# Row-wise largest magnitude on one core: two load queues, a ring of six slots, a finer tail and a direct last store

## The chip, the cores and the metric

One core of a Trainium2 chip runs the whole program. The metric is device time in microseconds (us) per execution. All times compared here are of the fast state, at full granted clock; experiments 8 and 9 are single runs of unknown state, read only for the stores inside them. "Span" is the time covered by the profiled execution; the time of an execution reads 1.7 to 1.9 us more (2.0 to 2.1 in experiment 4).

## The reference

```python
"x": np.random.randn(8192, 8192).astype(np.float32)

def reference(x):
    return np.linalg.norm(x, ord=np.inf, axis=1)      # largest |x| of each row
```

268 MB go in, 32 KB come out. There is one pass over the data and nothing is used twice.

## The kernel before

The 8192 rows form 64 tiles of 128 rows, one row per partition. Below, "row t" means tile t: 128 x 8192 values, 4 MB.

```python
COOLDOWN = ([[4096, 4096]] * 7 + [[4096, 2048, 2048]]
    + [[2048, 2048, 2048, 2048]] + [[2048, 2048, 1536, 1280, 1280]])
...
    chunks = [[n_cols]] * (T - len(COOLDOWN)) + COOLDOWN
...
pool = ctx.enter_context(tc.tile_pool(name="sbuf", bufs=5))
...
    for h, w in enumerate(ch):
        dst = res[:, t : t + 1] if len(ch) == 1 else partial[:, h : h + 1]
        nc.sync.dma_start(out=xt[:, off : off + w], in_=x_t[t, :, off : off + w])
        nc.vector.tensor_reduce(out=dst, in_=xt[:, off : off + w], ...,
            op=mybir.AluOpType.max, apply_absolute_value=True)
        off += w
    if len(ch) > 1:
        nc.vector.tensor_reduce(out=res[:, t : t + 1], in_=partial[:, : len(ch)], ...)
...
nc.tensor.transpose(res_t_psum, res, ident)           # 128 x 64 -> 64 x 128
nc.vector.tensor_copy(out=res_t, in_=res_t_psum)
nc.sync.dma_start(out=out.rearrange("(t p) -> t p", p=P), in_=res_t)
```

SP (SyncE) issues every load. The last ten rows come in pieces, so that little is left to reduce when the last bytes land. All results leave in one store at the end.

## Time and profile before

| | before |
|---|---|
| time, median | 634.63 us (634.53 to 634.78, 4 runs) |
| span | 632.9 us |
| one row arrives every | 9.71 us |
| one row takes VectorE (DVE) | 8.69 us |
| last reduce ends / span ends | 629.33 / 632.9 |

A list of DMA issues by output and input gives the time from issue to landing in its last column. For the final store of before it has:

```profile
out_dram<-res_t SPq DMA_DIRECT2D x1, 32.0 KB, 1.8
```

That is 64 rows of 512 B in 1.8 us.

### The profile page before, as it was taken

The numbers are of one execution on the slowest core, as the hardware profiler recorded it, in microseconds if no ns is written. First come the engines' busy times: TensorE is split into PE (matmuls) and PEld (weight loads), VectorE is DVE, ScalarE is ACT, GpSimd is POOL, SyncE is SP. The second block draws the span as 40 slices with busy tenths as digits, with TensorE's granted clock in tenths as the row PEclk, the third lists the DMA queues.
The fourth block names the chain that finished last, engine by engine and source line by source line (L and its number), as shares of the span: only waits on it lengthen the run. The fifth ranks groups of instructions, "written<-read, shape, count | busy, mean of one in ns | idle before, by whom it ended". The sixth has DMA issues, their size and how long they took to land.

```text
span 632.9 us, 294 instructions
## 1 busy us (share of the span) xinstructions
PE 0.4 (0%) x1; PEld 0.1 (0%) x1; DVE 558.9 (88%) x91; POOL 0.7 (0%) x6
## 2 busy tenths in 40 slices
PE   0000000000000000000000000000000000000000
PEld 0000000000000000000000000000000000000000
DVE  1988988988989889889898898898988989999997
POOL 0000000000000000000000000000000000000000
DMA  8999999999999999999999999999999999999995
GB/s 373 439 437 437 433 431 433 431 431 431 431 431 431 431 431 431 431 431 431 431 431 431 431 431 431 431 431 431 431 437 433 435 435 418 427 428 431 425 421 219
DMA packets 11602, 268.49 MB, mean 424 GB/s; under 512 B 1296, under 2 KB 1360, under 8 KB 1744
## 3 DMA queue, kind: packets, MB, share of 16 engines
q1 hardware_dynamic: 11600, 268.47, 98.9%
q14 instruction: 2, 0.02, 0.0%
HBM read 268.44 MB, written 0.03 MB: 424 GB/s over the span
## 4 chain that ended last, share of the span: by engine, by line
DMA 75%; DVE 24%; SPq 0%; issue 0%; PE 0%; DVEq 0%
DMA xt<-in_x_dram 75%; DVE res L59 15%; DVE partial L59 8%; SPq L55 0%; DVE res L68 0%; PE res_t_psum L78 0%; DVE res_t L80 0%; DVEq L59 0%
## 5 line engine op out<-in xcount | busy, mean ns | idle before, releaser
L59 DVE TENSOR_REDUCE res<-xt 128x1 f32<-128x8192 f32 x54 | 469.0, 8686 | 67.6 <-DMA xt<-in_x_dram 67.6
L59 DVE TENSOR_REDUCE partial<-xt 128x1 f32<-128x4096 f32 (+3 forms) x26 | 88.1, 3430 | 2.7 <-DMA xt<-in_x_dram 2.6
L68 DVE TENSOR_REDUCE res<-partial 128x1 f32<-128x2 f32 (+3 forms) x10 | 1.6, 156 | 0.3
L80 DVE COPY res_t<-res_t_psum 64x128 f32<-64x128 f32 x1 | 0.3, 283 | 0.6 <-PE res_t_psum L78 0.6
L78 PE MATMUL res_t_psum<-ident,res 128*64 128x128 f32 x1 | 0.4, 393 | 629.5 <-DVE res L68 629.5
masks.py:199 POOL TENSOR_SCALAR_AFFINE_SELECT ident<-ident 128x128 f32<-128x128 f32 x1 | 0.3, 292 | 0.1
L78 PEld LDWEIGHTS res_t_psum<-ident,res 128*64 128x64 f32 x1 | 0.1, 128 | 629.4 <-issue 629.4
masks.py:197 POOL MEMSET ident<- 128x128 f32 x1 | 0.2, 204 | 0.3 <-POOLq L96 0.3
L96 POOL MEMSET const-bfloat16-1.0<- 128x1 bf16 x1 | 0.1, 101 | 0.0
L96 POOL MEMSET const-uint8-127<- 128x1 uint8 x1 | 0.1, 101 | 0.0
L96 POOL MEMSET const-float32-0.0<- 128x1 f32 x1 | 0.1, 98 | 0.2 <-issue 0.2
L96 POOL MEMSET const-float32-1.0<- 128x1 f32 x1 | 0.1, 98 | 0.0
## 6 DMA issues: line engine op xcount, KB each, us to landing
xt<-in_x_dram SPq DMA_DIRECT2D x54, 4096.0 KB, 39.8
xt<-in_x_dram SPq DMA_DIRECT2D x15, 2048.0 KB, 38.7
xt<-in_x_dram SPq DMA_DIRECT2D x8, 1024.0 KB, 28.3
xt<-in_x_dram SPq DMA_DIRECT2D x2, 640.0 KB, 17.9
xt<-in_x_dram SPq DMA_DIRECT2D x1, 768.0 KB, 19.3
out_dram<-res_t SPq DMA_DIRECT2D x1, 32.0 KB, 1.8
```

The source lines that it names most:

```text
L59: nc.vector.tensor_reduce(out=dst, in_=xt[:, off : off + w], axis=mybir.AxisListType.X, op=mybir.AluOpType.max, apply_absolute_value=True,)
L68: nc.vector.tensor_reduce(out=res[:, t : t + 1], in_=partial[:, : len(ch)], axis=mybir.AxisListType.X, op=mybir.AluOpType.max,)
L78: nc.tensor.transpose(res_t_psum, res, ident)
L80: nc.vector.tensor_copy(out=res_t, in_=res_t_psum)
L96: nc = _bacc.Bacc("TRN2", target_bir_lowering=False, num_devices=1)
```

## The change

It has four parts. Whole rows are loaded alternately from SP and ACT (ScalarE). A ring of six slots replaces five buffers. Eight tail rows have pieces sized by a cost formula, down to 384 columns, and each row's last reduce takes the partial results in as extra columns. All but the last 128 results are stored early, and the last 128 go straight from the result column to memory, with no transpose.

```diff
+LOAD = (1.1815e-3, 0.043)
+REDUCE = (1.0417e-3, 0.060)
+FIRST = 384
+def tail_pieces(n_cols, big): ...      # sizes so that VectorE, with `big` columns in hand,
+                                       # is through just after the last landing
...
-    pool = ctx.enter_context(tc.tile_pool(name="sbuf", bufs=5))
+    ring = single.tile([P, RING + PAD], f32)              # six slots of 8192 columns
...
+    tail = tail_pieces(n_cols, R * n_cols)                # R = 1
+    for t in range(n_big):
+        queue = nc.sync if t % 2 == 0 else nc.scalar
+        queue.dma_start(out=buf, in_=x_big[t])
+        absmax(res_big[:, t, :], ...)
...
+    for t, widths in enumerate(tail):
+        for i, (w, at) in enumerate(zip(widths, spots)):
+            nc.sync.dma_start(out=ring[:, at : at + w], in_=x_tail[t, :, col : col + w])
...
+    store_early()                                         # transpose, copy, store of the other 63 rows
+    nc.sync.dma_start(
+        out=out_tail[n_tail - 1].rearrange("(p o) -> p o", o=1),
+        in_=res_tail[:, n_tail - 1 : n_tail],
+    )
```

## The prediction

> **What bounds the kernel now.** I read the page's slices first, then the groups of instructions, the waits, and the timeline of the start and of the end.
>
> ```profile
> span 632.9 us, 294 instructions
> ...
> DVE  1988988988989889889898898898988989999997
> ...
> DMA  8999999999999999999999999999999999999995
> ```
>
> The DMA row is full from the first slice to the last but one. VectorE (DVE) is nearly full, but its first slice shows a 1 and it becomes a steady 9 only at the end.
>
> ```profile
> L59 DVE TENSOR_REDUCE res<-xt 128x1 f32<-128x8192 f32 x54 | 469.0, 8686 | 67.6 <-DMA xt<-in_x_dram 67.6
> ```
>
> A whole row (128 x 8192, 4 MB) costs VectorE 8.69 us. The timeline tells how often one arrives (start, duration, what, idle before it):
>
> ```profile
> 12.88 8.69 DVE L59 TENSOR_REDUCE res<-xt 128x1 f32<-128x8192 f32 x1 [12.88 <-DMA xt<-in_x_dram]
> 22.58 8.69 DVE L59 TENSOR_REDUCE res<-xt 128x1 f32<-128x8192 f32 x1 [1.01 <-DMA xt<-in_x_dram]
> 32.29 8.69 DVE L59 TENSOR_REDUCE res<-xt 128x1 f32<-128x8192 f32 x1 [1.02 <-DMA xt<-in_x_dram]
> ```
>
> Every 9.71 us, so 432 GB/s, and VectorE idles 1.0 us a row. **Loads bound the kernel**, with VectorE only 10% behind. The end, from the same view:
>
> ```profile
> 592.30 4.42 DVE L59 TENSOR_REDUCE partial<-xt 128x1 f32<-128x4096 f32 x1 [0.36 <-DMA xt<-in_x_dram]
> ...
> 602.09 8.81 DVE L59 TENSOR_REDUCE partial<-xt 128x1 f32<-128x4096 f32 x3 [0.35 <-DMA xt<-in_x_dram]
> ...
> 611.12 8.86 DVE L59 TENSOR_REDUCE partial<-xt 128x1 f32<-128x2048 f32 x4
> ...
> 620.21 8.92 DVE L59 TENSOR_REDUCE partial<-xt 128x1 f32<-128x2048 f32 x5
> 629.17 0.16 DVE L68 TENSOR_REDUCE res<-partial 128x1 f32<-128x5 f32 x1
> 629.44 0.13 PEld L78 LDWEIGHTS res_t_psum<-ident,res 128*64 128x64 f32 x1 [629.44 <-issue]
> 629.47 0.39 PE L78 MATMUL res_t_psum<-ident,res 128*64 128x128 f32 x1 [629.47 <-DVE res L68]
> 629.90 0.28 DVE L80 COPY res_t<-res_t_psum 64x128 f32<-64x128 f32 x1 [0.58 <-PE res_t_psum L78]
> 630.21 0.55 SPq L81 DMA_DIRECT2D out_dram<-res_t  x1
> ```
>
> From 602.09 VectorE never waits. The loads' data run dry at about 625.3 to 626.4 (moved bytes by windows), the last 1280 columns have landed at 626.9, and their reduce begins at 627.66. After the last reduce ends (629.33), transpose and copy take 0.9 us, the store 1.8 us from issue to landing, the close 0.8 us. So from the last landing to the end of the span there are 6.0 us.
>
> Two cost lines follow. A row in two loads takes 602.09 - 592.30 = 9.79 us against 9.71 for one, so **a row in n loads takes 9.63 + 0.08 n**. On VectorE the chain shows rows of 2, 3, 4 and 5 pieces at 8.76, 8.82, 8.88 and 8.94 us: **8.64 + 0.06 n**.
>
> One wait matters for the limits of issue:
>
> ```profile
> SPq L55 <- DMA xt<-in_x_dram: 109.8, 72, 9.7
> ```
>
> 72 is 80 loads less 8: from the ninth on, each load waits for the landing of one eight before it. So at most eight loads are outstanding. Pieces are reduced while other pieces of the same tile are still loading, so waits follow the columns and not the whole tile; I expect the same of the one large ring.
>
> **What the Trainium skill says.** (1) "DMA: Bandwidth & Descriptors", section "Queues, rings and completion order": SP and ACT own one row of rings each on the same 16 engines, and each engine goes round-robin between rows that have work, a packet at a time. The trace before has one load queue, so no run shows this yet; its packets are one 32 KB row each, eight an engine for a 4 MB load. (2) Same page, "Issuing engines are not separate DMA queues": a second issuing engine saves only issue time. The trace agrees that issue costs nothing here: about 0.4 us for a load of 9.71 us, issued 39.8 us ahead. (3) "VectorE: DVE Perf Modes", "The perf-mode tier table": tensor_reduce has only the one-element-a-cycle mode. 8192 at 0.96 GHz is 8.53 us, the trace has 8.69; so no piece size buys rate. (4) First page, "Specifications": transfers under 512 B are read-modify-writes. The new last store writes 128 values of 4 bytes each; the old one writes 64 rows of 512 B in 1.8 us.
>
> **The change, part by part.**
>
> *Ring of six instead of five.* One more row in flight. Loads already never pause: worth 0.
>
> *Two queues for 56 whole rows.* Same bytes, same 32 KB packets, so I keep 9.72 us a row (mean from 12.88 to the last whole row at 527.99, 53 rows). But if the engines alternate packets, rows 2k and 2k+1 share the bandwidth and **land as a pair** every 19.4 us instead of one every 9.7. Row 55 still lands near 12.88 + 55 x 9.72 = 547.4; row 54 only one packet (1.2 us) earlier, 546.2, where now it would be 9.7 earlier. Mid-stream this is free: a pair takes 17.4 us of 19.4. At the end VectorE is left with two rows, not one, when the tail starts.
>
> *The tail.* Working the sizing function by hand gives 8 rows in 2, 2, 2, 2, 3, 4, 6 and 13 pieces: 34 in place of 26, the last of 384 columns. All are loaded by SP alone. Loads: 8 x 9.63 + 34 x 0.08 = 79.8 us, so the last lands at 547.4 + 79.8 = 627.2, against 626.9 now: ten more loads in all at 0.08 are 0.8 us, less chance pauses. VectorE: 8 x 8.64 + 34 x 0.06 = 71.2 us; the separate small reduce (0.2 us a row) goes into the last piece.
>
> If VectorE had just one whole row in hand at 547.4, it would be through at 547.4 + 8.7 + 71.2 = 627.3: just with the loads; that is what the sizes aim at. With the pair it starts row 54 at 546.2 and ends at 546.2 + 17.4 + 71.2 = **634.8**, 7.6 us after the last landing, whatever the last piece's size.
>
> *The end.* Transpose, copy and store of the other 63 x 128 results lie beside the last row. Left are a hand-over (0.05), the store of 4-byte pieces, which I take at 2.0 us (estimate from the 1.8 of now), and 0.8 to close: 2.85 us in place of 3.5. ACT's copies and any table load are off the path.
>
> Sum with pairs: 634.8 + 2.85 = 637.6 of span; timed runs are 1.8 over the span now (634.7 against 632.9), so **639.4 us**. VectorE becomes the bound of the end and takes back what the finer pieces and the shorter store gain (about 3.5 us from the last landing).
>
> **Rivals.** *A: pairs, rate unchanged:* 639.4, weight 0.45. For it: the skill's round-robin, and both queues always hold at least two rows of work. *B: loads are served one after another* (an engine takes a whole load's eight packets before switching, or the queues settle half a period apart). Then the design works: last landing 627.2, last reduce of 396 elements 0.6, then 2.85: 630.6, timed **632.4**. Weight 0.25; what speaks for it is that sizes this carefully fitted were presumably checked. *C: pairs, but a second queue fills the fixed 0.08 us a load* (more work ready on each engine): up to 56 x 0.08 = 4.5 us earlier, VectorE's end with it: about **636**. Weight 0.2; against it, the DMA row is already full. *D: two streams disturb each other, or the ring's waits go wrong* (a load waiting for more than its own columns): 645 and up; weight 0.06. The rest is B and C together, 628 to 629.
>
> **Range and chances.** The weighted middle lies between A and C: 637. B sets the low end and A with some slip the high one: 631 to 641. Two per cent is 12.7 us; only D gets there above, and nothing below: 528 us of the loads can't shrink by that much.
>
> **What would show it.** Pairs: the first reduce starts at 21 to 23 us instead of 12.9; from then waits come in turns, a long one (1 to 2 us) before SP's rows and nearly none before ACT's; time to landing of whole loads grows; VectorE shows no wait from about 546 to the end. Serial service would show the first reduce at 12.9 and a 1 us idle before each row. The rate reads off the start of row 54's reduce, 546 if unchanged, 542 under C. The last landing should be near 627, and the last store near 2.0 us. I am wrong if VectorE waits for loads within the last 30 us, or if the loads' rate moves by more than 1%.

## The result, and the profile after

The changed kernel takes **644.68 us** (644.62 to 645.04, 4 runs) against 634.63: ratio 1.0158, 95% interval 1.0144 to 1.0173. Ratios and intervals here are those of the record, which compares fast runs of both kernels; they are not quite the ratios of the medians quoted. The stated range ended at 641.

The page of the changed kernel:

```profile
span 643.3 us, 316 instructions
...
DVE  0588898888998888988888988888988888999994
...
DMA  9999999999999999999999999999999999999990
```

VectorE is now empty in the first slice and half empty in the second. In the last slice the DMA engines show 0, and VectorE is not full either. So part of the end belongs to nobody's work.

The timeline of the start (start, duration, what, idle before):

```profile
0.73 78.34 ACTq L104 DMA_DIRECT2D ring<-in_x_dram  x6
...
0.74 89.15 SPq L104 DMA_DIRECT2D ring<-in_x_dram  x7
...
22.55 17.28 DVE L92 TENSOR_REDUCE res_big<-ring 128x1 f32<-128x8192 f32 x2 [22.55 <-DMA ring<-in_x_dram]
41.99 17.28 DVE L92 TENSOR_REDUCE res_big<-ring 128x1 f32<-128x8192 f32 x2 [2.16 <-DMA ring<-in_x_dram]
```

Rows now land in pairs. The first reduce starts at 22.55 instead of 12.88. Then two rows are reduced back to back ("x2", 17.28 us), and VectorE waits 2.16 us before the next pair. The trace also records landings, the moments at which a load's 16 completions come in (read from the packed trace; no view prints them): row 0 is in at 22.53 and row 1 at 22.70. A pair comes every 19.44 us, the same rate as a row every 9.71.

The timeline of the end:

```profile
547.22 17.28 DVE L92 TENSOR_REDUCE res_big<-ring 128x1 f32<-128x8192 f32 x2 [2.16 <-DMA ring<-in_x_dram]
564.41 8.74 DVE L92 TENSOR_REDUCE ring<-ring 128x1 f32<-128x4096 f32 x2
...
626.27 8.08 DVE L92 TENSOR_REDUCE ring<-ring 128x1 f32<-128x768 f32 x11
...
634.39 0.57 DVE L92 TENSOR_REDUCE res_tail<-ring 128x1 f32<-128x396 f32 x1
634.98 0.36 SPq L140 DMA_DIRECT2D out_dram<-res_tail  x1
```

The last pair is ready at 547.2. VectorE then never waits for a load again; the last reduce ends at 634.96. By the record of landings the last load is in at 627.6. So VectorE is 7.4 us behind the loads.

The second surprise comes after that. SP's own waits (line and what ended the wait: us in total, times, longest) and the list of DMA issues show it:

```profile
SPq L167 <- DMA out_dram<-res_tail: 6.8, 1, 6.8
```
```profile
out_dram<-res_tail SPq DMA_DIRECT2D x1, 0.5 KB, 7.3
```

The store of 512 bytes takes 7.3 us from issue to landing, where 32 KB took 1.8. Its packets move between 635.8 and 636.0, 9 ns each. But the 16 completions that count it as landed arrive one at a time from 637.8 to 642.2, 0.3 us apart on average.

So from before to after, the last reduce ends 5.6 us later (629.33 to 634.96). The time from there to the end of the span grows from 3.5 to 8.3 us (the store and the close of the program). Together that is 10.4 us, the whole difference of the spans.

### The profile page after: what moved, and what is told of

It reads as the page before. It is cut to its first block, busy times and chain, and to the rows that moved or that the text cites. A ratio compares the mean times of both kernels' runs of the same rounds, so it can differ in the third digit from the quotient of the medians.

```text
span 643.3 us, 316 instructions
## 1 busy us (share of the span) xinstructions
PE 0.8 (0%) x2; PEld 0.2 (0%) x2; DVE 554.2 (86%) x90; ACT 1.8 (0%) x3; POOL 0.7 (0%) x6
## 4 chain that ended last, share of the span: by engine, by line
DMA 73%; DVE 22%; issue 4%; DVEq 0%
DMA ring<-in_x_dram 73%; DVE res_big L92 14%; DVE ring L92 5%; DVE res_tail L92 4%; DVEq L92 0%
## 5 line engine op out<-in xcount | busy, mean ns | idle before, releaser
L92 DVE TENSOR_REDUCE res_big<-ring 128x1 f32<-128x8192 f32 x56 | 483.8, 8681 | 80.7 <-DMA ring<-in_x_dram 80.7
L92 DVE TENSOR_REDUCE ring<-ring 128x1 f32<-128x4096 f32 (+15 forms) x26 | 45.9, 1832 | 0.0
L92 DVE TENSOR_REDUCE res_tail<-ring 128x1 f32<-128x4097 f32 (+4 forms) x8 | 25.5, 3210 | 0.0
```

The source lines that it names most:

```text
L92: nc.vector.tensor_reduce(out=dst, in_=src, axis=mybir.AxisListType.X, op=mybir.AluOpType.max, apply_absolute_value=True,)
```

## The experiments

Theory after the comparison: two separate costs, the pair in hand at the start of the tail, and the form of the last store. All twelve kernels computed the right result.

**1. One queue.**

```diff
-        queue = nc.sync if t % 2 == 0 else nc.scalar
+        queue = nc.sync
```

> The changed kernel with every load issued from SP; ring, tail and direct last store stay. Theory (two rows that land as a pair leave VectorE with two rows instead of one when the tail begins): first reduce at 12.9 instead of 22.6, VectorE idle 1.1 us before each whole row, last reduce ends near 627.8 instead of 634.96, the last store still takes 7.3 us; timed 637.5. Rival (the backlog comes from the tail's own sizes or from the ring, not from the queues): the end of the last reduce stays near 635 and the time near 644.7.

Measured: 639.07 us (638.38 to 639.14), ratio 1.0071. Its timeline:

```profile
13.01 8.69 DVE L92 TENSOR_REDUCE res_big<-ring 128x1 f32<-128x8192 f32 x1 [13.01 <-DMA ring<-in_x_dram]
22.70 8.69 DVE L92 TENSOR_REDUCE res_big<-ring 128x1 f32<-128x8192 f32 x1 [1.01 <-DMA ring<-in_x_dram]
...
627.92 0.57 DVE L92 TENSOR_REDUCE res_tail<-ring 128x1 f32<-128x396 f32 x1
```

Rows come singly again and the last reduce ends at 628.5, 6.5 us sooner. The store still takes 7.1 us. The time is 1.6 us above the expected 637.5: 0.7 us is the last reduce, and the other three runs had spans some 0.7 us longer than the profiled one. The ring and the tail sizes are cleared; the queues make the backlog.

**2. The last 128 results as one row.**

```diff
-    nc.sync.dma_start(out=out_tail[n_tail - 1].rearrange("(p o) -> p o", o=1),
-                      in_=res_tail[:, n_tail - 1 : n_tail])
+    nc.tensor.transpose(ps_last, res_tail[:, n_tail - 1 : n_tail], ident)
+    nc.vector.tensor_copy(out=line_last, in_=ps_last)
+    nc.sync.dma_start(out=out_tail[n_tail - 1 :], in_=line_last)
```

> The changed kernel with both queues, but the last 128 results go through a transpose and a copy and leave as one row of 512 B. Theory (the store of 128 separate 4-byte values itself is slow, 7.3 us): it lands in about 1.8 us, 0.9 us come back for transpose and copy, so timed 640.1. Rival (the last store waits for something else, such as the stores issued before it or memory still busy with loads): it still lands about 7 us after its issue, timed 645 to 646.

Measured: 639.58 us (639.5 to 639.69), ratio 1.0079. Its timeline:

```profile
634.29 0.57 DVE L92 TENSOR_REDUCE res_tail<-ring 128x1 f32<-128x396 f32 x1
...
635.63 0.23 SPq L144 DMA_DIRECT2D out_dram<-line_last  x1
```

The span ends at 637.7, 2.1 us after this issue. Stores issued earlier are as in the changed kernel, so the rival falls: it is the form of the store, not what precedes it. The detour by PE (TensorE) costs 0.8 us, and from the issue of the store to the end there are 2.1 us instead of 8.3.

**3. Both.**

> The changed kernel with one queue and with the row store. If the two costs are separate and add, it takes both savings: last reduce ends at 627.8, 3.5 us from there to the end of the span, timed 633.0, which is 1.6 us under the kernel before. If they overlap (one hides behind the other), it is no better than the better of the two alone.

Measured: **633.06 us** (632.89 to 633.24), ratio 0.9976 (0.9961 to 0.9991). Alone the two edits save 5.6 and 5.1 us, together 11.6, a little over their sum of 10.7: they are separate and add. The 0.9 us over the sum stays unexplained. What is left of the change (ring, tail sizes, early store) is worth 1.6 us over the kernel before.

**4. Two queues, but a tail for two rows in hand.**

```diff
-    tail = tail_pieces(n_cols, R * n_cols)
+    tail = tail_pieces(n_cols, 2 * n_cols)
```

> The changed kernel, both queues and the direct last store kept, but the tail is sized for two whole rows in hand instead of one: 16 tail rows (eight of them whole, 42 loads in all, all from SP) after 48 rows on two queues. Theory (VectorE only lacks time to work off the second row): pair 46 and 47 lands at 469.6, VectorE needs 17.3 + 140.8 us from there, so the last reduce ends near 628 instead of 634.96; timed 638 to 639, like the run with one queue. Rival (two queues cost time by themselves, by disturbed loads): the time stays above 643.

Measured: 638.08 us (637.7 to 638.53), ratio 1.0055. Its timeline:

```profile
469.40 17.28 DVE L92 TENSOR_REDUCE res_big<-ring 128x1 f32<-128x8192 f32 x2 [2.14 <-DMA ring<-in_x_dram]
...
547.12 8.69 DVE L92 TENSOR_REDUCE res_tail<-ring 128x1 f32<-128x8192 f32 x1 [0.29 <-DMA ring<-in_x_dram]
...
627.65 0.57 DVE L92 TENSOR_REDUCE res_tail<-ring 128x1 f32<-128x396 f32 x1
```

After the last pair (469.40) VectorE works off the second row, and at 547.12 it waits for a load again. The last reduce ends at 628.2. Two queues as such cost nothing that could be seen (638.08 beside 639.07 with one); what costs is a tail that is too short for the pair.

**5. The kernel before, with two queues for whole rows alone.**

```diff
-            nc.sync.dma_start(
+            queue = nc.scalar if len(ch) == 1 and t % 2 else nc.sync
+            queue.dma_start(
```

> The kernel before with one thing of the change: whole rows issued from SP and ACT in turn (five buffers, its own tail and its own single store stay). Theory: rows 52 and 53 land as a pair at 528, VectorE then has 8.6 us more than before to do and none of the 2.6 us of waits that it has now: the last reduce ends 5.9 us later, timed about 640.5. Rival (the pair does harm only with the ring or the new tail): 634.7, unchanged.

Measured: 640.30 us (640.27 to 640.32), ratio 1.009. Its last small reduce,

```profile
634.81 0.16 DVE L69 TENSOR_REDUCE res<-partial 128x1 f32<-128x5 f32 x1
```

ends at 634.97, 5.6 us later than in the kernel before (expected 5.9). So the ring and the new tail aren't needed for the harm.

**6. Out of step, first try.** ACT's first load was to wait for a reduce on the first 1280 columns of row 0. This kernel and the next have the row store.

```diff
+        if t == 0:
+            f = 1280
+            queue.dma_start(out=buf[:, :f], in_=x_big[t][:, :f])
+            queue.dma_start(out=buf[:, f:], in_=x_big[t][:, f:])
+            absmax(ring[:, n_cols : n_cols + 1], buf[:, :f])      # one column of ACT's first slot
```

> Both queues, tail of the change, row store; but ACT's first load has to wait for a small reduce on the first 1280 columns of row 0, so that its rows run about half a period behind SP's. Compare with the row store and two queues in step (639.6) and with one queue (633.1). Theory (rows in hand when the tail begins decide): rows land about 10 us apart, singly; but SP begins the tail while row 55 is still half to load, so VectorE has about a row and a half in hand: last reduce near 632, timed near 637. If only landing in pairs matters: 633. If two queues as such matter: 639.6.

Measured: 641.12 us (641.03 to 641.21), ratio 1.0103. That is none of the three expected values. Its timeline:

```profile
14.87 1.49 DVE L92 TENSOR_REDUCE ring<-ring 128x1 f32<-128x1280 f32 x1 [14.87 <-DMA ring<-in_x_dram]
...
531.61 34.47 DVE L92 TENSOR_REDUCE res_big<-ring 128x1 f32<-128x8192 f32 x4 [2.13 <-DMA ring<-in_x_dram]
565.99 8.73 DVE L92 TENSOR_REDUCE ring<-ring 128x1 f32<-128x4096 f32 x2
```

The edit missed its aim: another of ACT's loads, which had nothing to wait for, was issued first, at 0.73, and the one that waits only at 16.4. So the offset came out wrong. VectorE finished the whole rows at 566.0, later than the 564.4 of the changed kernel. It also left a finding: the 1280-column piece (0.6 MB) landed at 14.84 and the 4 MB row on the other queue at 14.68. Both have 128 packets in the trace (a packet is one partition's row), of 5 KB and of 32 KB. So the engines took **one packet from each queue in turn, a small one counting as much as a large one**.

**7. Out of step, mended.** One column in each of ACT's first three slots is written by VectorE first.

```diff
+            for s in (3, 5):
+                nc.vector.tensor_copy(out=ring[:, s * n_cols : s * n_cols + 1],
+                                      in_=ring[:, n_cols : n_cols + 1])
```

> The half-period run mended. There ACT did not wait: a later row of its queue was issued at 0.73 us instead, so the offset was not the intended one, and when SP's last whole row landed VectorE had even a little more in hand (18.7 us against 17.3 in step). Now one column of each of ACT's first three slots is written by VectorE first, so that no ACT load can start before 5 to 7 us. Expected: first reduce of a row at 16 to 18, the next at 27 to 29, then rows singly, 8.5 and 11 us apart; the last whole row lands at 552 to 553 with only itself in hand, last reduce near 632.5, timed 637.1 (4.6 over the last reduce, as in the best run with this store). If pairing has nothing to do with it: 639.6, as in step with this store.

Measured: 636.27 us (636.0 to 636.6), ratio 1.0021. Its timeline:

```profile
4.73 1.49 DVE L92 TENSOR_REDUCE ring<-ring 128x1 f32<-128x1280 f32 x1 [4.73 <-DMA ring<-in_x_dram]
...
535.11 25.87 DVE L92 TENSOR_REDUCE res_big<-ring 128x1 f32<-128x8192 f32 x3 [2.15 <-DMA ring<-in_x_dram]
560.90 8.73 DVE L92 TENSOR_REDUCE ring<-ring 128x1 f32<-128x4096 f32 x2
```

With SP alone at work, the same piece lands at 4.7 instead of 14.8. The picture in the expectation is not exact. By the record of landings rows came singly, but 6 and 13 us apart (29.8, 36.0, 49.2, 55.4 and so on) and not 8.5 and 11. So VectorE, at 8.7 us a row, mostly reduced them two by two; once it waited 21.5 us, until 107.5, and then reduced eighteen without a pause, and why it waited there is not shown. At the end the last whole row landed at 550.9 and was through at 560.9, so little but itself was in hand, as expected, and the time falls 3.3 us below two queues in step. One sum covers these kernels, which VectorE bounds at the end (experiment 2 too): **the last reduce ends 70.5 us after the whole rows are through**.

| kernel | whole rows reduced at | last reduce ends | difference |
|---|---|---|---|
| out of step, mended | 560.90 | 631.44 | 70.54 |
| the changed kernel | 564.41 | 634.96 | 70.55 |
| out of step, first try | 565.99 | 636.53 | 70.54 |

VectorE has no wait in these 70.5 us. So with this tail only an earlier start helps, down to the loads' own end.

**8 and 9. Forms of the small store.** After the kernel of experiment 3, stores into scratch memory, each waiting for the one before.

```diff
+    for name, (parts, width, pitch) in scratch.items():
+        s = nc.dram_tensor(name, (parts, pitch), f32, kind="Internal").ap()
+        nc.vector.memset(forms, 0.0)
+        nc.sync.dma_start(out=s[:, :width], in_=forms[:parts, :width])
```

> Eight stores into scratch memory at the end of the previous kernel, each waiting for the one before, so that nothing else moves. Reading: time from issue to landing. 128 values of 4 B packed into 512 B: 7.3 us, twice (first and last). Theory 1 (small writes into the same few bytes of memory wait for one another): 128 values 512 B apart land in about 2 us, 64 B apart in between, 16 packed values (one an engine) in about 2.5. Theory 2 (each small write is slow wherever it goes): all 128-value forms land in about 7 us whatever their distance. Controls: 128 rows of 64 B packed 2 to 4 us, 128 rows of 512 B about 2 us, one row of 512 B about 1.8. The time of the whole kernel means nothing here.

> Second set of stores into scratch memory, each waiting for the one before; read from issue to landing. Known: 128 values of 4 B packed 7.1 us, 64 B apart 1.4, 16 packed (one per DMA engine) 1.3, 128 rows of 64 B packed 1.4. Theory 1a (small writes that share a 64 B block with another write wait for one another, each wait a fixed time): 8 B, 16 B and 32 B apart fall in steps (about 16, 4 and 2 writes a block less one), packed rows of 16 B and 32 B are slow too, about as 16 B and 32 B apart. Theory 1b (it is the number of values in 512 B): only the packed form is slow, everything else under 2 us. 32 and 64 packed values (2 and 4 an engine): between 1.3 and 7.1 in proportion to their number under both.

Two lists of DMA issues, of the first set and of the second (last column: us from issue to landing):

```profile
s<-forms SPq DMA_DIRECT2D x2, 0.5 KB, 1.4
...
s_few<-forms SPq DMA_DIRECT2D x1, 0.1 KB, 1.3
s_8192B<-forms SPq DMA_DIRECT2D x1, 8.0 KB, 1.4
...
s_again<-forms SPq DMA_DIRECT2D x1, 0.5 KB, 7.1
```
```profile
f_64of<-forms SPq DMA_DIRECT2D x1, 0.2 KB, 6.5
...
f_128of<-forms SPq DMA_DIRECT2D x1, 0.5 KB, 7.0
```

All forms, from issue to the last completion in the record of landings:

| stored | us |
|---|---|
| 128 values of 4 B, packed | 7.1, 7.0 |
| 64 / 16 values of 4 B, packed | 6.5 / 1.3 |
| 128 values of 4 B, 8 B / 16 B / 32 B apart | 2.6 / 1.4 / 1.6 |
| 128 values of 4 B, 64 B or 512 B apart | 1.4 |
| 128 pieces of 16, 32 or 64 B, packed | 1.4 |
| 128 rows of 512 B | 1.5 |
| one row of 512 B from one partition | 1.1 |

Small writes as such are not slow: 128 of them 16 B apart take 1.4 us. 64 and 128 of them are slow when they lie closer than that. So distance decides, as in theory 1 of the first set, and theory 2 falls; but 64 B apart is as fast as 512 B and not in between, and that close writes wait for one another is argued, not shown. Both refinements in the second set are wrong in part. 16 B and 32 B apart are fast, against 1a. 8 B apart is slower (2.6 us) and 64 packed values are nearly as slow as 128, against 1b and against proportion. What the memory does with such writes, and why 16 packed values are fast, stays open. Two packed stores issued while loads still ran, one of 128 values (8.4 us) and one of 32 (4.7 us), are left out of the table, since they were not alone.

**10. A direct store in pieces of 64 B.** The tail is sized for two rows in hand, as in experiment 4, and its 16 rows are laid so that a partition holds 16 neighbouring results; one queue.

```diff
-    x_tail = x[split:].rearrange("(t p) m -> t p m", p=P)
+    x_tail = x[split:].rearrange("(p t) m -> t p m", p=P)
...
+    nc.sync.dma_start(out=out_tail, in_=res_tail)         # out_tail: "(p t) -> p t", 128 x 64 B
```

> One queue; 16 tail rows laid so that a partition holds 16 neighbouring rows; all 2048 tail results then leave straight from the result tile as 128 pieces of 64 B, with no transpose. Theory (only small writes that share a 64 B block are slow): the store lands in about 1.4 us, 2.3 us from the last reduce to the end of the span against 2.9 with transpose: timed 632.5, best so far. Rival (the rows of a tail load are then 512 KB apart in memory[...]): tail loads slow down, time well above 634.7.

Measured: 632.80 us (632.68 to 632.9), ratio 0.997. From the end of the last reduce to the end of the span there are 2.5 us, against 2.9 with the row store. The idea of a store with no transpose was sound; only the 4-byte form was not. The rival (slow loads of rows 512 KB apart) is refuted: two of these tail rows,

```profile
538.00 8.69 DVE L92 TENSOR_REDUCE res_tail<-ring 128x1 f32<-128x8192 f32 x1 [1.03 <-DMA ring<-in_x_dram]
547.73 8.69 DVE L92 TENSOR_REDUCE res_tail<-ring 128x1 f32<-128x8192 f32 x1 [1.05 <-DMA ring<-in_x_dram]
```

arrive 9.73 us apart, like any others.

**11. Two rows a load.** From experiment 3, with `R = 2`: 24 loads of 8 MB, then 16 tail rows.

> One queue and row store as in the run that was best so far (633.1), but two rows a load for the first 48 rows (8 MB a load, 64 KB a partition; three slots), then a 16-row tail sized for two rows in hand. 66 loads instead of 90. If the fixed cost of a load is 0.08 us whatever its size, that is 1.9 us less: 631.2. If it belongs to the 32 KB packets, of which as many are moved, nothing: 633. The row that lands as a double must not hurt here, since the tail is sized for it: last reduce within 1 us of the last landing.

Measured: **631.49 us** (631.39 to 631.65), ratio 0.9951 (0.9936 to 0.9965). Its timeline:

```profile
22.79 17.22 DVE L92 TENSOR_REDUCE res_big<-ring 128x2 f32<-128x16384 f32 x1 [22.79 <-DMA ring<-in_x_dram]
42.14 17.22 DVE L92 TENSOR_REDUCE res_big<-ring 128x2 f32<-128x16384 f32 x1 [2.13 <-DMA ring<-in_x_dram]
```

Two rows come every 19.35 us instead of 19.43: one fixed cost of 0.08 us saved. In all 1.6 us are saved beside experiment 3, of 1.9 expected. The expectation took it that as many packets of 32 KB are moved, and that is not so: the trace has 3072 packets of 64 KB in these 24 loads. Loads and packets fell together, so whether the 0.08 us belongs to a load or to its 128 packets is not shown. Landing in twos does no harm, since the tail is sized for two: the last reduce ends at 626.85, 0.1 us after the last load is in.

**12. Two rows a load and the 64 B store.** The edits of 10 and 11 together.

> Two rows a load, one queue, and the 64 B store straight from the result tile together. If their gains add: 0.3 us less from the last reduce to the end than two rows a load alone, so 631.2; same or slower if the wide store's 512 KB spacing costs in the loads.

Measured: **631.18 us** (630.63 to 631.82), ratio 0.9938 (0.9921 to 0.9954): 3.6 us under the kernel before. It is 0.3 us under number 11, as expected, but the runs of the two overlap, so this last step is not shown by the times.

## Why the prediction was wrong

- **What bounds, and the pair: right.** Rival A was what happened. First reduce expected at 21 to 23, measured 22.55; row 54 expected at 546.2, its reduce began at 547.22; last landing 627.2 expected, 627.6 measured; last reduce 634.8 expected, 634.96 measured. VectorE showed no wait from 547 on, as foretold. That the last reduce fits so closely is in part luck: row 54 came 1.0 us late, since the rows of a pair land 0.2 us apart and not 1.2, while the pair took 17.2 us instead of 17.4 and the tail 70.55 instead of 71.2.
- **The step that failed** is in "The end": "the store of 4-byte pieces, which I take at 2.0 us (estimate from the 1.8 of now)". It measured 7.3 us. A's sum was 637.6 of span, the page says 643.3. Of the 5.7 us between them, 5.3 are this store; the close took 1.0 instead of 0.8, and the last reduce ended 0.2 later. The skill's page had been cited for a read-modify-write of small transfers, but no cost was put to it: an estimate from 512 B rows was carried over to 4 B pieces, and the one operation of the change that the trace of before did not contain went unmeasured.
- **The weights were a smaller error.** B (serial service) had 0.25 and C (fixed cost hidden by a second queue) 0.2, which drew the centre from 639.4 to 637 and the upper end to 641. Neither occurred. Pairs landed within 0.2 us of each other, and a pair took 19.44 us, just two single rows, so the 0.08 us per load was not hidden. Experiment 11 shows that it is saved by fewer and larger loads instead.
- **"Ring of six: worth 0", "ten more loads are 0.8 us".** The second is right in size: in experiment 3, with the two costs gone, the last load is in at 627.69, 0.8 us after that of the kernel before (626.88). The last reduce ended at 628.4, 0.9 us before that of the kernel before, and the time gained was 1.6 us. The ring was never run alone, so its worth is not shown.
- **The gain hoped for** by the change at the end (finer pieces, no transpose) was thus paid back twice: 7.4 us of backlog behind the loads, and some 5.3 us in a store that skipped a 0.8 us detour.

## What to carry to other kernels

When loads are the bound and the consuming engine is nearly as slow, ask how many tiles it will have in hand when the last stage begins: two queues deliver the same bytes per second, but in pairs, and a tail sized for one tile is then too short. Measure an operation that the old kernel doesn't contain before trusting a number from its nearest relative; a store of 4-byte values side by side is no small version of a store of rows. If results must leave without a transpose, lay them so that each partition holds at least 16 B of neighbouring output (16, 32 and 64 B a partition landed in 1.4 us here).

## What the Trainium skill lacked or had wrong

- "DMA: Bandwidth & Descriptors", "Specifications", has under 512 B a read-modify-write but not what such a store costs: 128 values of 4 B take 7.1 us packed, 2.6 us 8 B apart, 1.4 to 1.6 us 16 B or more apart, beside 1.5 us for 128 rows of 512 B. Whether the slow ones are read-modify-writes no run shows.
- Same page, "Queues, rings and completion order": the round-robin between queues is seen. The page gives 9 to 17 descriptors as typical of a packet; in this trace a packet is one row of one partition, and the queues alternate at that grain (rows 0 and 1 landed 0.2 us apart). It doesn't say that shares then go by number of packets and not by bytes: 0.6 MB in 5 KB packets landed at 14.84 us, beside 4 MB in 32 KB packets at 14.68, and at 4.7 us when alone.
- Same page, "Issuing engines are not separate DMA queues", has a second issuing engine save issue time and no more. It can also cost: tiles land in pairs, which took 5.6 us in the kernel before and about as much in the changed one.
- Same page, "Latency and other measured facts", has rates by row pitch only for copies between HBM tensors, 207 GB/s at 512 KiB against 214 for a padded pitch, and none for loads into SBUF. Loads of 128 rows of 32 KB at a pitch of 512 KB showed no slowing: 9.73 us a row, as for whole rows at the same place in experiment 1.
- No page that was read has the fixed cost of a load from SP in a queue that always has more to do: 0.08 us for a load of 128 packets (by load or by packet is not shown).
